# First modulation piece turned ahead of the first inverse rms, which stays in PSUM: the opening of a two-layer diffusion block

## The chip, the cores and the metric

The kernel runs on one core of one Trainium2 chip. Its engines are TensorE (PE, with PEld for its weight loads), VectorE (DVE), ScalarE (ACT), GpSimd (POOL) and SyncE (SP, which issues most transfers). The metric is the device time of one execution in microseconds; less is better.

## The reference

Two layers over 512 latent tokens and 256 context tokens of width 1024, batch 1. Only the opening of layer 0 matters here:

```
sh1, sc1, g1, sh2, sc2, g2 = split(silu(c) @ w_mod[0] + b_mod[0], 6)        # the same with c_ctx for the context
h  = rmsnorm(x,   norm_mix[0]) * (1 + sc1)  + sh1
hc = rmsnorm(ctx, norm_mix[0]) * (1 + csc1) + csh1
p  = concat(h, hc) @ w_in_ab[0]        # 1024 -> 2560, then gates and convolutions
```

All of it is float32. After the opening come the rest of the input projection, two convolutions and the output projection, the ConvFFN of layer 0, windowed attention with a sink, the ConvFFN of layer 1 and a final RMSNorm.

## The kernel before, in words

Activations lie transposed: `x` is eight tiles of 128 channels by 776 columns (512 latent, 8 empty, 256 context; `segs` are the two non-empty stretches). Every product is made three times, with each operand split into a high part (a copy in the matmul's type, by ACT) and a low part (the rest, by DVE): low weight times high activation, high times low, high times high (the three lines of `mm3`, L185 to L187 before, L188 to L190 after). `split` makes both parts, `weights` loads a 128x1024 piece of weights and splits it, `wide_gemm` multiplies a piece with the two stretches of one or more of the eight activation tiles.

PSUM is four slots of 128x1024 numbers. `start` is the opening:

- It squares and sums the eight `x` tiles (ACT and DVE). `inverse` turns the sums into means on PE (L303), reads them on ACT (`rv`) and makes the inverse root by Newton steps of small DVE instructions. DVE puts it on a diagonal (`rd`, L325) and PE spreads it over the partitions into a slot (L335).
- It makes the scale and shift of the 16 column blocks of layer 0 in four pieces. A piece (`mod_piece`) is four loads (`wmod`), 32 small matmuls into one quarter of a slot (L238), an ACT copy (`modsb`, L243), a transpose on PE (L244, here called the turn), a second ACT copy (L246), a DVE addition of the bias (`mod`, L247) and the gain (`make_gain`, L278). Piece q serves the activation tiles 2q and 2q+1.
- It normalises and modulates each tile k (`mod_in`): DVE multiplies x by the inverse rms (`xr`, L348); ACT applies gain and shift in two instructions (latent and context) and, for k of 2 and more, casts the result to the high part; DVE makes the low part. For k below 2 ACT writes the high part directly (L357) and DVE makes the full value itself (L358).
- With each tile it advances three output slots (`sl`) by three pieces of `w_in`: 18 matmuls for a tile.

The code is written in program order; a scheduling layer then lays the instructions out engine by engine, each engine executes its own list strictly in order, and semaphores carry the dependences between lists. It also orders accesses of different engines to one slot whose columns do not overlap (rows below show such waits). `issue_after` pins an instruction behind another in that layout. In the kernel before, the inverse rms goes into `sl[0]` (columns 0 to 775), is copied to SBUF (`r`, L444) by ACT, and the pieces use the fourth slot `ms` alone (`acc` at columns 0 to 127, the turn at 768 to 895).

## Time and profile before

| | |
|---|---|
| median of 3 runs | 1461.03 us (1460.87 to 1461.33) |
| the profiled execution | 1462.82 us, span of its instructions 1461.0 us |
| PE busy | 1421.9 us, 97% of the span |
| DVE, ACT, POOL busy | 74%, 44%, 12% |
| chain that ended last | PE 82%, DVE 7%, DMA 5%, ACT 3% |

The span runs from the first to the last instruction of the profiled execution. The busy share of an engine counts its instructions; the chain that ended last is followed back from the last instruction through whatever released each step. Times within the trace are counted from the start of the span.

### The profile page before, as it was taken

To read this page: it belongs to the slowest core of one execution; us is meant where nothing else is said; L and a number is where in the kernel's file an instruction comes from. 1 tells how busy PE (TensorE), PEld (TensorE's weight loads), DVE (VectorE), ACT (ScalarE), POOL (GpSimd) and SP (SyncE) were. 2 spreads that over 40 slices of the span, in tenths; PEclk is the share of its full clock that TensorE was granted. 3 is DMA by queue.
4 is the path that set the end of the run, shared out by engine and by line. 5 is a ranking of instruction groups with operands and counts; after the bars stand their busy time and mean duration, and the time that the engine had idled before them with its cause. 6 is when DMAs were issued, how large, how long until landed. Compare 5 with 4: busy or idle time off the path is not lost.

```text
span 1461.0 us, 24131 instructions
## 1 busy us (share of the span) xinstructions
PE 1421.9 (97%) x9470; PEld 1249.1 (85%) x9470; DVE 1083.3 (74%) x1750; ACT 649.8 (44%) x1105; POOL 181.3 (12%) x427
## 2 busy tenths in 40 slices
PE   5999999999999999999999999999999999999997
PEld 3888888888888888888888878867799999999897
DVE  6699998689878557565534679787767977777676
ACT  5422224473223223123213365687765745545455
POOL 0000001112222212112212110243200000000000
PEclk9999999999999999999999999999999999999999
DMA  9325433036787767847725315264532444444441
GB/s 375 113 71 174 159 116 130 30 101 204 212 223 190 218 194 197 250 156 185 162 98 100 111 59 159 67 134 110 122 116 97 157 152 158 146 156 157 148 130 68
DMA packets 80546, 215.69 MB, mean 148 GB/s; under 512 B 10032, under 2 KB 10160, under 8 KB 80304
## 3 DMA queue, kind: packets, MB, share of 16 engines
q1 hardware_dynamic: 63408, 174.29, 36.1%
q0 software_dynamic: 17024, 39.86, 13.0%
q8 instruction: 74, 1.21, 0.3%
q14 instruction: 40, 0.33, 0.1%
HBM read 209.39 MB, written 41.94 MB: 172 GB/s over the span
## 4 chain that ended last, share of the span: by engine, by line
PE 82%; DVE 7%; DMA 5%; ACT 3%; issue 2%; POOL 1%; SPq 0%; DVEq 0%; ACTq 0%
PE slot L185 20%; PE slot L186 20%; PE slot L187 19%; DMA wraw<-in_w_down 3%; PE av L1091 2%; DVE wlo L167 2%; PE pt L1081 2%; PE s L1062 2%; PE av L185 2%; PE av L186 2%; PE av L187 1%; ACT whi L166 1%; PE slot L220 1%; PE slot L224 1%; PE slot L221 1%
## 5 line engine op out<-in xcount | busy, mean ns | idle before, releaser
L185 PE MATMUL slot<-h,wlo 128*128 128x256 f32 (+1 forms) x1152 | 382.5, 334 | 2.8 <-DVE ub L582 1.2
L186 PE MATMUL slot<-h,whi 128*128 128x256 f32 (+1 forms) x1152 | 382.5, 333 | 0.2 <-DVE h L362 0.2
L187 PE MATMUL slot<-h,whi 128*128 128x256 f32 (+1 forms) x1152 | 382.7, 332 | 0.0
L166 ACT CAST whi<-wraw 128x1024 fp32r<-128x1024 f32 (+2 forms) x249 | 219.9, 892 | 240.8 <-PE slot L187 88.1
L167 DVE TENSOR_TENSOR wlo<-wraw,whi 128x1024 fp32r<-128x1024 f32 (+2 forms) x249 | 254.4, 1027 | 72.2 <-ACT whi L166 71.5
L185 PEld LDWEIGHTS slot<-h,wlo 128*128 128x128 f32 x1152 | 216.5, 188 | 29.0 <-issue 2.0
L186 PEld LDWEIGHTS slot<-h,whi 128*128 128x128 f32 x1152 | 217.0, 188 | 23.1 <-DVE h L362 0.5
L187 PEld LDWEIGHTS slot<-h,whi 128*128 128x128 f32 x1152 | 217.0, 188 | 21.8
L382 DVE SCALAR_TENSOR_TENSOR cf<-slot,par,cf 128x775 f32<-128x775 f32 (+1 forms) x92 | 92.6, 1009 | 97.8 <-ACT cf L380 97.7
L185 PE MATMUL slot<-gh,wlo 128*128 128x512 f32 (+1 forms) x435 | 148.8, 344 | 2.1 <-ACT gh L166 1.1
L186 PE MATMUL slot<-gl,whi 128*128 128x512 f32 (+1 forms) x435 | 147.9, 341 | 0.0
L187 PE MATMUL slot<-gh,whi 128*128 128x512 f32 (+1 forms) x435 | 147.6, 340 | 0.0
L380 ACT ACTIVATE cf<-slot,par 128x776 f32<-128x776 f32 (+1 forms) x46 | 41.4, 901 | 192.8 <-PE slot L187 188.7
L590 DVE SCALAR_TENSOR_TENSOR cacc<-ub,par,cacc 128x783 f32<-128x783 f32 x120 | 118.4, 1035 | 0.3
L266 DVE CUSTOM_DVE_ANT_0 junk<-wmod,cb 128x1024 bf16<-128x1024 f32 x80 | 97.5, 1218 | 22.1 <-DMA wmod<-in_wmt 20.5
L372 DVE SCALAR_TENSOR_TENSOR x<-slot,mod,x 128x256 f32<-128x256 f32 (+1 forms) x139 | 80.9, 612 | 40.9 <-PE slot L187 40.4
L185 PEld LDWEIGHTS slot<-gh,wlo 128*128 128x128 f32 x435 | 81.4, 188 | 12.7 <-ACT gh L166 1.3
L187 PEld LDWEIGHTS slot<-gh,whi 128*128 128x128 f32 x435 | 81.8, 188 | 9.8
L186 PEld LDWEIGHTS slot<-gl,whi 128*128 128x128 f32 x435 | 81.9, 188 | 9.6 <-DVE mod L247 0.2
L1069 DVE CUSTOM_DVE_ANT_0 sm<-s,mask,nsink 128x640 f32<-128x640 f32 (+1 forms) x58 | 46.6, 819 | 13.9 <-PE pt L1081 10.7
L860 ACT ACTIVATE sgf<-cf 128x776 f32<-128x776 f32 (+1 forms) x44 | 32.6, 742 | 53.6 <-DVE cf L382 53.6
L1072 ACT ACTIVATE sm<-sm,nm 128x513 f32<-128x513 f32 (+1 forms) x64 | 50.0, 785 | 10.7 <-DVE nm L1069 7.1
(333 smaller groups left out, 2873.3 us busy)
## 6 DMA issues: line engine op xcount, KB each, us to landing
s<-in_w_up POOLq DMA_DIRECT2D x114, 256.0 KB, 5.5
wmod<-in_wmt SPq DMA_DIRECT2D x56, 512.0 KB, 4.6
wraw<-in_w_up SPq DMA_DIRECT2D x50, 512.0 KB, 4.2
wmod<-in_wm SPq DMA_DIRECT2D x40, 512.0 KB, 5.1
wraw<-in_w_up SPq DMA_DIRECT2D x57, 256.0 KB, 2.9
wraw<-in_w_down SPq DMA_DIRECT2D x48, 256.0 KB, 3.1
wraw<-in_w_in SPq DMA_DIRECT2D x20, 512.0 KB, 3.9
wraw<-in_w_down SPq DMA_DIRECT2D x32, 320.0 KB, 3.0
```

Of the source, the lines that this page charges most:

```text
L166: self.act_mark = self.nc.scalar.copy(hi, src)
L167: self.mark = self.nc.vector.tensor_tensor(lo, src, hi.bitcast(F32), op=ALU.subtract)
L185: mm(out, lo, xh, start=first, stop=False)
L186: mm(out, hi, xl, start=False, stop=False)
L187: self.product = mm(out, hi, xh, start=False, stop=last)
L266: nc.vector.tensor_tensor_reduce(junk, w, self.cb[:, c, :], 1.0, 0.0, ALU.mult, ALU.add, col)
L372: self.nc.vector.scalar_tensor_tensor(self.x[k][:, lo:hi], acc, self.mod[:, l, chunk * 8 + k, c:c + 1], self.x[k][:, lo:hi], op0=ALU.mult, ...
L380: nc.scalar.activation(acc[:, :n], u[:, :n], AF.Copy, scale=w[:, 1:2])
L382: nc.vector.scalar_tensor_tensor(acc[:, o], u[:, i], w[:, j:j + 1], acc[:, o], op0=ALU.mult, op1=ALU.add)
L590: self.tapped = nc.vector.scalar_tensor_tensor(acc, ub[:, t:t + CB_N], w[:, t:t + 1], acc, op0=ALU.mult, op1=ALU.add)
L1069: scored = nc.vector.tensor_tensor_reduce(sm[:, :n], s[:, SEQ - nl:SEQ + CTX], mk, -SCALE, nsink[:, hd:hd + 1], ALU.add, ALU.min, nm)
L1072: self.scored = scored, nc.scalar.activation(sm[:, :n + 1], sm[:, :n + 1], AF.Exp, scale=-1.0, bias=nm, accum_out=z)
```

## The change

What it does, part by part:

- `mod_piece` turns into the columns that it accumulated in, 896 to 1023 of `ms`, and takes an instruction behind which its matmuls are pinned.
- The means and then the spread inverse rms lie in `ms` too, at columns 0 to 775; the copy `r` is gone, and `mod_in` reads the rms from PSUM. The spread is pinned behind the turn of piece 0.
- The first three pieces of `w_in` are no longer split in one go. ACT casts the first behind `rv` and the other two behind the second copy of piece 0. The low part of the first is made by DVE behind `rd`, that of the second by DVE between the tiles 0 and 1, that of the third by GpSimd.
- Piece 1 stands in the code behind the modulation of tile 1, piece 2 behind the products of tile 1, piece 3 behind those of tile 3. Before, piece 1 stood ahead of tile 0 and both others behind the products of tile 1.
- The products of a tile stand directly behind its modulation. Before, both tiles of a pair were modulated ahead of the products of either.

The core of the diff:

```diff
@@ -164,7 +164,10 @@
     def split(self, src, hi, lo):
 
         self.act_mark = self.nc.scalar.copy(hi, src)
-        self.mark = self.nc.vector.tensor_tensor(lo, src, hi.bitcast(F32), op=ALU.subtract)
+        self.low(src, hi, lo)
+
+    def low(self, src, hi, lo, eng=None):
+        self.mark = (eng or self.nc.vector).tensor_tensor(lo, src, hi.bitcast(F32), op=ALU.subtract)
 
     def weights(self, dram, n=1024, into=None):
...
@@ -224,7 +227,7 @@
                     self.nc.tensor.matmul(s[:, lo:hi], wh, xl, start=False, stop=k == len(rhs) - 1)
 
 
-    def mod_piece(self, l, lo, hi, at, dram, acc, tr, room):
+    def mod_piece(self, l, lo, hi, at, dram, acc, tr, room, after=None):
 
         nc = self.nc
         for quarter in range(4):
@@ -232,18 +235,19 @@
                 yield
             w = room(quarter)
             nc.sync.dma_start(w, dram[quarter])
-            for kk in range(2):
-                k = quarter * 2 + kk
-                for j in range(4):
-                    nc.tensor.matmul(
-                        acc[32 * j:32 * j + 2, :], self.csil[:, k, :], w[:, kk, j * P:(j + 1) * P],
-                        start=k == 0, stop=k == KT - 1,
-                    )
+            with self.tc.issue_after(after.ins) if after else nullcontext():
+                for kk in range(2):
+                    k = quarter * 2 + kk
+                    for j in range(4):
+                        nc.tensor.matmul(
+                            acc[32 * j:32 * j + 2, :], self.csil[:, k, :], w[:, kk, j * P:(j + 1) * P],
+                            start=k == 0, stop=k == KT - 1,
+                        )
         sb = self.tmp.tile([P, P], F32, name="modsb", tag="r", bufs=1)
         nc.scalar.copy(sb, acc)
-        nc.tensor.transpose(tr, sb, self.ident)
+        self.mod_turned = nc.tensor.transpose(tr, sb, self.ident)
         sb = self.tmp.tile([P, P], F32, name="modsb", tag="r", bufs=1)
-        nc.scalar.copy(sb, tr)
+        self.mod_copied = nc.scalar.copy(sb, tr)
         nc.vector.tensor_tensor(
...
@@ -430,31 +434,51 @@
             self.square_in(k, 0, T)
         sl = [self.slot() for _ in range(3)]
         ms = self.slot()
-        nc.vector.memset(ms[:, 0:P], 0.0)
-
-        def piece(q):
+        nc.vector.memset(ms[:, 896:1024], 0.0)
+
+        def piece(q, after=None):
             room = lambda _: ph.tile([P, 2, 512], F32, name="wmod", tag="wmod", bufs=14)
-            for _ in self.mod_piece(0, 0, 16, 2 * q, a["wm0"][q], ms[:, 0:P], ms[:, 768:768 + P], room):
+            for _ in self.mod_piece(0, 0, 16, 2 * q, a["wm0"][q], ms[:, 896:1024], ms[:, 896:1024], room, after):
                 pass
             self.make_gain(0, 0, 1, self.p("nmix")[:, 0:8], 2 * q, 2 * q + 2)
 
-        piece(0)
-        rp = self.rstd(self.ss, segs, self.ones2, sl[0], eng=nc.vector, pool=ph)
-        r = self.tmp.tile([P, T], F32, name="r", tag="ss", bufs=1)
-        nc.scalar.copy(r, rp)
-        room = [[ph.tile([P, DM], F32R, name=t) for t in ("whi0", "wlo0")], None, None]
-        first = [self.weights(a["w_in"][m], into=room[m]) for m in range(3)]
-        piece(1)
+        chunks = [c for lo, hi in segs for c in range(lo, hi, P)]
+        y = self.inverse(self.ss, chunks, self.ones2, ms[:, 0:2 * len(chunks)], nc.vector)
+        piece(0, self.stats)
+        d = ph.tile([P, len(chunks), P], F32, name="rd", tag="rd")
+        rd = nc.vector.tensor_tensor(
+            d, self.ident.unsqueeze(1).broadcast_to(d.shape), y.unsqueeze(2).broadcast_to(d.shape), op=ALU.mult)
+        with self.tc.issue_after(self.mod_turned.ins):
+            for lo, hi in segs:
+                i, j = lo // P, (hi - lo) // P
+                nc.tensor.matmul(ms[:, lo:hi], self.onesm, d[:, i:i + j, :].rearrange("p n c -> p (n c)"), start=True, stop=True)
+        r = ms[:, 0:T]
+
+        first, raws = [], []
+        for m in range(3):
+            raws.append(self.wts.tile([P, 1024], F32, name="wraw", tag="wraw", bufs=3))
+            nc.sync.dma_start(raws[m], a["w_in"][m])
+            first.append([ph.tile([P, DM], F32R, name=t) for t in ("whi0", "wlo0")] if m == 0 else
+                         [self.wts.tile([P, 1024], F32R, name=t, tag=t, bufs=3) for t in ("whi", "wlo")])
+            with self.tc.issue_after((self.mod_copied if m else self.means).ins):
+                nc.scalar.copy(first[m][0], raws[m])
+        with self.tc.issue_after(rd.ins):
+            self.low(raws[0], *first[0])
+        self.low(raws[2], *first[2], nc.gpsimd)
         h = self.new_h()
         for q in range(4):
             for k in (2 * q, 2 * q + 1):
-                self.mod_in(h, k, r, 0, 0, 0, segs)
-            for k in (2 * q, 2 * q + 1):
+                with self.tc.issue_after(self.mark.ins) if k == 1 else nullcontext():
+                    self.mod_in(h, k, r, 0, 0, 0, segs)
+                if k == 0:
+                    with self.tc.issue_after(self.mark.ins):
+                        self.low(raws[1], *first[1])
+                if k == 1:
+                    piece(1)
                 for s, w in zip(sl, first):
                     self.wide_gemm(s, w, h, segs, [k])
-            if q == 0:
-                piece(2)
-                piece(3)
+            if q < 2:
+                piece(q + 2)
         return h, sl
```

`rstd` also loses its argument `pool`, and `mod_in` calls the new `low` for k below 2.

What the layout makes of it is shown at three places. A row is an instruction of one engine in its order, with its line, result and operands, its size, and the semaphores that it waits for.

PE, from the end of piece 0 on. Before (`rd`, `onesm`: the spread; `modsb`: the turn; `wmod`: a piece's matmuls; `wlo`: a low product):

```order
L335 MATMUL slot0_102<-rd_207,onesm_86 128x512 [waits DVE_49,Activation_49]
L335 MATMUL slot0_102<-rd_207,onesm_86 128x256
L244 MATMUL slot3_105<-ident_84,modsb_177 128x128 [waits DMAHW1_49,Activation_49]
L238 MATMUL slot3_105<-wmod_231,csil_94 2x128 [waits DMAHW1_49,Activation_49]
L238 MATMUL slot3_105<-wmod_231,csil_94 2x128 x7
L238 MATMUL slot3_105<-wmod_241,csil_94 2x128 [waits DMAHW2_49]
L238 MATMUL slot3_105<-wmod_241,csil_94 2x128 x7
L238 MATMUL slot3_105<-wmod_251,csil_94 2x128 [waits DMAHW3_49]
L238 MATMUL slot3_105<-wmod_251,csil_94 2x128 x7
L185 MATMUL slot0_102<-h_278,wlo0_214 128x512 [waits Activation_49]
L185 MATMUL slot1_103<-h_278,wlo_222 128x512 [waits DVE_49]
L185 MATMUL slot2_104<-h_278,wlo_228 128x512 [waits DVE_49]
```

After:

```order
L248 MATMUL slot3_105<-ident_84,modsb_200 128x128 [waits DMAHW1_49,Activation_49]
L454 MATMUL slot3_105<-rd_207,onesm_86 128x512 [waits DVE_49,Activation_49]
L454 MATMUL slot3_105<-rd_207,onesm_86 128x256
L188 MATMUL slot0_102<-h_228,wlo0_214 128x512 [waits Activation_49]
L188 MATMUL slot2_104<-h_228,wlo_224 128x512 [waits Pool_49]
L189 MATMUL slot0_102<-h_229,whi0_213 128x512 [waits DVE_49]
L190 MATMUL slot0_102<-h_228,whi0_213 128x512
L188 MATMUL slot0_102<-h_228,wlo0_214 128x256 [waits Activation_49]
L189 MATMUL slot0_102<-h_229,whi0_213 128x256
```

The turn of piece 0 has gone ahead of the spread; the 32 matmuls of piece 1, of which 24 stood ahead of the first low product, are gone from here; the second product of tile 0 is that of the third weight piece, which waits for GpSimd.

DVE, between the low parts of the first two tiles and the later tiles (`xr_440` is tile 2, `xr_490` tile 4; after, `xr_391` and `xr_488`; `modsb_387` comes from piece 2, `modsb_484` from piece 3). Before:

```order
L362 TENSOR_TENSOR h_279<-ht_296,h_278 128x776 [waits DVE_49,Activation_49]
L348 TENSOR_TENSOR xr_440<-x2_69,r_211 128x776 [waits DMAHW2_49]
L362 TENSOR_TENSOR h_281<-ht_304,h_280 128x776 [waits DVE_49,Activation_49]
L348 TENSOR_TENSOR xr_447<-x3_70,r_211 128x776 [waits DMAHW3_49]
L247 TENSOR_TENSOR mod_92<-modsb_274,par_66 128x2x4 [waits Activation_49]
L278 SCALAR_TENSOR_TENSOR gain_93<-mod_92,par_66 128x4 [waits DVE_49]
L348 TENSOR_TENSOR xr_490<-x4_71,r_211 128x776 [waits DMAHW4_49,Activation_49]
L348 TENSOR_TENSOR xr_497<-x5_72,r_211 128x776 [waits DMAHW5_49,Activation_49]
L167 TENSOR_TENSOR h_283<-ht_442,h_282 128x776 [waits Activation_49]
L167 TENSOR_TENSOR h_285<-ht_449,h_284 128x776 [waits Activation_49]
```

After:

```order
L251 TENSOR_TENSOR mod_92<-modsb_387,par_66 128x2x4 [waits Activation_49]
L352 TENSOR_TENSOR xr_391<-x2_69,slot3_105 128x776 [waits DMAHW2_49,PE_49]
L352 TENSOR_TENSOR xr_416<-x3_70,slot3_105 128x776 [waits DMAHW3_49]
L282 SCALAR_TENSOR_TENSOR gain_93<-mod_92,par_66 128x4 [waits DVE_49]
L170 TENSOR_TENSOR wlo_605<-wraw_602,whi_604 128x1024 [waits DMAHW5_49,Activation_49]
L170 TENSOR_TENSOR h_233<-ht_393,h_232 128x776 [waits Activation_49]
L170 TENSOR_TENSOR h_235<-ht_418,h_234 128x776 [waits Activation_49]
L251 TENSOR_TENSOR mod_92<-modsb_484,par_66 128x2x4 [waits Activation_49]
L352 TENSOR_TENSOR xr_488<-x4_71,slot3_105 128x776 [waits DMAHW4_49,DVE_49,PE_49]
L352 TENSOR_TENSOR xr_513<-x5_72,slot3_105 128x776 [waits DVE_49]
```

Before, the products with the rms wait for no PE instruction and those of tiles 4 and 5 stand ahead of the `mod` of piece 2. After, those of tiles 2 and 3 stand behind the `mod` of piece 2, those of tiles 4 and 5 behind the `mod` of piece 3, and the first of each pair waits for PE.

PE, at the turn of piece 3. Before (`h_286` and `h_287` are the high and low part of tile 4) it stands among the products of tile 4:

```order
L186 MATMUL slot2_104<-h_285,whi_227 128x256
L187 MATMUL slot2_104<-h_284,whi_227 128x256
L185 MATMUL slot0_102<-h_286,wlo0_214 128x512 [waits Activation_49]
L185 MATMUL slot1_103<-h_286,wlo_222 128x512
L185 MATMUL slot2_104<-h_286,wlo_228 128x512
L244 MATMUL slot3_105<-ident_84,modsb_433 128x128 [waits Activation_49]
L186 MATMUL slot0_102<-h_287,whi0_213 128x512 [waits DVE_49]
L187 MATMUL slot0_102<-h_286,whi0_213 128x512
L185 MATMUL slot0_102<-h_286,wlo0_214 128x256
```

After (`h_235` is the low part of tile 3, `h_236` and `h_237` are tile 4):

```order
L190 MATMUL slot2_104<-h_234,whi_223 128x512
L188 MATMUL slot2_104<-h_234,wlo_224 128x256
L189 MATMUL slot2_104<-h_235,whi_223 128x256
L190 MATMUL slot2_104<-h_234,whi_223 128x256
L248 MATMUL slot3_105<-ident_84,modsb_481 128x128 [waits Activation_49]
L188 MATMUL slot0_102<-h_236,wlo0_214 128x512 [waits Activation_49]
L188 MATMUL slot1_103<-h_236,wlo_219 128x512
L188 MATMUL slot2_104<-h_236,wlo_224 128x512
L189 MATMUL slot0_102<-h_237,whi0_213 128x512 [waits DVE_49]
```

The turn now stands behind the last product of tile 3, and the first product of tile 4 is next to it.

## Rows read from the trace of the kernel before

**Rows 1.** Windows: length; busy PE, PEld, DVE, ACT, POOL (instructions); granted clock; DMA.

```profile
28.85:57.90 29.05, 29.05 (x272) 24.78 (x272) 14.04 (x21) 16.01 (x27) 0.56 (x12) 1.00 0.56 211
57.90:1461.00 1403.10, 1381.33 (x9053) 1216.73 (x9051) 1050.98 (x1688) 617.21 (x1057) 180.56 (x411) 1.00 0.48 142
```

**Rows 2.** Waits of PE from 57.9 us on: total, times, longest.

```profile
PE slot L303 <- DVE ss L296: 2.1, 2, 2.0
```

**Rows 3.** Timeline of the opening, DVE and ACT: start, length, instruction, idle before.

```profile
17.01 0.18 ACT L306 ACTIVATE rv<-slot 128x6 f32<-128x6 f32 x1 [2.54 <-PE slot L303]
...
20.72 2.17 ACT L166 CAST whi<-wraw 128x1024 fp32r<-128x1024 f32 x2
22.80 0.81 ACT L444 COPY r<-slot 128x776 f32<-128x776 f32 x1
...
20.71 3.49 DVE L167 TENSOR_TENSOR wlo<-wraw,whi 128x1024 fp32r<-128x1024 f32 x3
...
26.26 2.52 ACT L357 ACTIVATE h<-xr,mod,gain 128x512 fp32r<-128x512 f32 x4 [2.49 <-DVE gain L278]
27.84 0.96 DVE L362 TENSOR_TENSOR h<-ht,h 128x776 fp32r<-128x776 f32 x1
```

**Rows 4.** Timeline of PE in the opening.

```profile
16.90 3.59 PE L238 MATMUL slot<-wmod,csil 128*2 128x128 f32 x64
20.94 1.82 PE L335 MATMUL slot<-rd,onesm 128*128 128x512 f32 x4 [0.45 <-ACT modsb L243]
22.60 0.27 PE L244 MATMUL slot<-ident,modsb 128*128 128x128 f32 x1
...
28.85 0.50 PE L186 MATMUL slot<-h,whi 128*128 128x512 f32 x1 [0.21 <-DVE h L362]
31.41 0.85 PE L185 MATMUL slot<-h,wlo 128*128 128x512 f32 x3
34.74 1.93 PE L238 MATMUL slot<-wmod,csil 128*2 128x128 f32 x64
40.91 1.93 PE L238 MATMUL slot<-wmod,csil 128*2 128x128 f32 x64
```

**Rows 5.** Instructions of the piece matmuls and the spread: shortest, median, longest in ns.

```profile
L238 PE MATMUL slot<-wmod,csil x256: 270/273/418, 16.9 to 42.6; 128*2 128x128 f32 x128
L335 PE MATMUL slot<-rd,onesm x4: 379/486/960, 20.9 to 22.4; 128*128 128x512 f32 x2, 128*128 128x256 f32 x2
```

**Rows 6.** Timeline from the turn of piece 1 to the casts it serves, all engines.

```profile
32.10 0.27 PE L244 MATMUL slot<-ident,modsb 128*128 128x128 f32 x1
32.40 0.27 ACT L246 COPY modsb<-slot 128x128 f32<-128x128 f32 x1 [3.37 <-PE slot L244]
32.70 0.17 DVE L247 TENSOR_TENSOR mod<-modsb,par 128x8 f32<-128x8 f32 x1 [1.27 <-ACT modsb L246]
33.10 2.52 ACT L360 ACTIVATE ht<-xr,mod,gain 128x512 f32<-128x512 f32 x4 [0.43 <-DVE gain L278]
35.53 1.57 ACT L166 CAST h<-ht 128x776 fp32r<-128x776 f32 x2
```

**Rows 7.** The tile-wide instructions of that chain: shortest, median, longest in ns.

```profile
L348 DVE TENSOR_TENSOR xr<-x,r x8: 956/962/969, 24.1 to 41.2; 128x776 f32<-128x776 f32 x8
L166 ACT CAST h<-ht x6: 824/836/838, 35.5 to 50.2; 128x776 fp32r<-128x776 f32 x6
L609 DVE TENSOR_TENSOR z<-slot,gc x4: 960/965/967, 118.8 to 204.6; 128x776 f32<-128x776 f32 x4
```

**Rows 8.** The one tile-wide GpSimd instruction, and DVE's taps that started beside or behind it.

```profile
L596 POOL TENSOR_TENSOR cs<-cacc x1: 1882/1882/1882, 190.7 to 190.7; 128x783 f32<-128x783 f32 x1
L590 DVE SCALAR_TENSOR_TENSOR cacc<-ub,par,cacc x3: 1020/1021/1997, 191.5 to 194.3; 128x783 f32<-128x783 f32 x3
```

**Rows 9.** Timeline of SP's queue in the opening: the fourth and later pieces of `w_in`.

```profile
28.28 15.48 SPq L172 DMA_DIRECT2D wraw<-in_w_in  x4
```

**Rows 10.** The `wraw` tiles of the first 60 us: from issue to landing.

```profile
DMA to landing us min/median/max: 3.5/9.1/11.2
```

## What is predicted, before the run

> **What bounds the kernel now.** I read the windows first, because the change touches only the opening. From 28.85 us, the first product of a high part, to 57.90 PE is busy 29.05 us of 29.05, and after that it stands still for only 1403.10 - 1381.33 = 21.8 us in all [rows 1]; there its longest single wait is 2.0 us [rows 2], at the end of a chain that has to start later when the opening ends later. So the rest of the kernel is a line of PE work: a microsecond that PE loses or wins in the opening reaches the end, and there is hardly idle time behind it in which to lose it again. What counts is when PE can start its full run, how much of its work lies before that, and whether the run stays unbroken.
>
> The timeline of DVE and ACT shows why the run starts at 28.85. `rv` is read at 17.01; DVE then makes the inverse root, the diagonal and, from 20.71, three low parts of weights in 3.49 us, and only then, at 24.2, `xr`; ACT writes h from 26.26 and DVE its low part at 27.84 to 28.80 [rows 3]. PE meanwhile does piece 0 (16.90, 3.59 us), the spread (20.94, 1.82 us), the turn (22.60), the 32 matmuls of piece 1 in its waits, and three low products; the two later pieces, at 34.74 and 40.91, are 1.93 us of the unbroken run [rows 4].
>
> **The head of the opening.** Up to `rv`, nothing moves. The matmuls of piece 0 now wait for `rv` (17.01 + 0.18) because both lie in one slot: 17.25 instead of 16.90, and with the same 3.59 us they end at 20.85. ACT's copy (0.27, row of the turn of piece 1 [rows 6]) ends at 21.15, the turn at about 21.6 (0.27 at the pace of 22.60; I give it 0.4, since the shared pace of PE was still lower here, below), the second copy at 21.9. The spread follows at 22.0 and takes between 1.3 and the 1.82 us of [rows 4]; I take 1.5: 23.5. `xr` reads the slot; DVE products that read a slot take 965 ns against 962 without [rows 7], so reading it costs nothing and the 0.81 us copy `r` [rows 3] is saved: 24.5. ACT's two instructions for one tile are half of 2.52 us [rows 3], to 25.8; the low part takes 0.96, and with the handovers PE has its first high product at 26.9, **1.95 us earlier** than 28.85. The low part of the first weights (1.2 us of the 3.49) lies under the wait for the turn, that of the second behind the low part of tile 0, where PE has the 1.6 us of the other two slots to do.
>
> GpSimd's low part is the unknown of the head. ACT casts the second and third piece from 21.9 (2.17 us for two [rows 3]), to 24.1. The nearest row is the one tile-wide GpSimd instruction, 1882 ns for 783 columns [rows 8]: 2.46 us for 1024, so 26.6, under the 26.9. It stands second on PE, and all of PE is queued behind it. Below, the bound is DVE's own 1.2 us, which changes nothing; above, I double it, since a DVE instruction that ran beside that GpSimd row took 1997 ns instead of 1020 [rows 8] and the harm may fall on either side: 29.0, 2.1 us late. I take 2.46.
>
> The Trainium skill ("GPSIMD Engine Reference", section 8, Key points) says that GpSimd shares its SBUF interfaces with VectorE and that the two contend where VectorE reads two SBUF inputs. The 1997 ns agree; by that rule it is DVE's low part of tile 0 that stretches, by at most 1 us, and the sum would be 11.0 instead of 10.0.
>
> What PE had done by then also changes. Before, piece 1 and three low products lay ahead of the run; now it has two low products. Left over are 32 matmuls, 1.86 us (64 steps from 34.74 to 36.60 [rows 4]), and one low product, a third of 0.69 = 0.23 us (0.85 us for three with the tail [rows 4]). The head is worth -1.95 + 2.09 = **+0.15 us**: the earlier start only pays for work that used to lie in the waits.
>
> **The stalls in the run.** Before, a piece ran through behind PE's back: the turn stood among products, and `xr` of the next tiles needed nothing from PE. Now the products with the rms read `ms`, where the pieces live. The rows of the order show what follows: `xr` of tiles 2 and 3 stands on DVE behind the `mod` of piece 2, `xr` of tiles 4 and 5 behind the `mod` of piece 3, and the matmuls of pieces 1 and 3 wait for DVE.
>
> - Piece 2 waits for the second copy of piece 1, whose turn now stands directly ahead of it: turn 0.27, copy 0.27, two handovers, less the 0.13 that the turn takes of PE anyway: **0.5 us**.
> - At the end of piece 2 PE waits for its copy, turns (0.27), and waits for the second copy (0.27), `mod` (0.17) [rows 6] and two `xr` (0.96 each [rows 7]) before piece 3 may write the slot. 0.25 of tail, 0.27, 0.27, 0.27, 0.17, 1.9, with six handovers of 0.03 to 0.05 (32.37 to 32.40, 32.67 to 32.70 [rows 6]), less 0.13: **3.3 us**. Piece 3 itself (1.86) covers part of the rest of the chain: four ACT instructions 2.52, a cast 0.83 [rows 6, 7], from the end of the first `xr`, 3.3 against 0.95 + 1.86: **0.5 us**. Three low products then cover 0.69 of the 0.96 of the low part: **0.3 us**.
> - The turn of piece 3 stands behind the last product of tile 3, and the first product of tile 4 needs the whole chain from it: turn 0.27, copy 0.27, `mod` 0.17, `xr` 0.96, four ACT instructions 2.52, cast 0.83, handovers 0.15, less 0.13 = **5.0 us** in which PE has nothing, and **0.3 us** for the low part again.
>
> Tiles 5 to 7 then come in time: their ACT and DVE work per pair, 2.52 + 1.57, is less than the 6.3 us that PE needs for two tiles (29.05 us less two pieces, over eight tiles, is 3.15 for one). The sum of the stalls is 0.5 + 3.3 + 0.5 + 0.3 + 5.0 + 0.3 = 9.9 us, with the head **+10.0 us**.
>
> The Trainium skill ("PSUM — Partial Sum Buffer", section "PSUM bank collisions raise a hardware error") says that the hardware does not arbitrate between two engines in one bank and that semaphores must guard PSUM by bank rather than by address. No run here shows what the hardware does without the waits; the order shows that the waits are there although the columns are apart, which is this rule at work. If guarding went by address alone, `xr` of tiles 2 to 5 would run ahead and the sum would be about the head's 0.15.
>
> The transfers do not move: SP's list is the same, the pieces 2 and 3 are needed at about 35.5 and 41, near 34.74 and 40.91. One cast is new on the path: the fourth piece of `w_in`, ahead of ACT's work on tile 2 at 38.6. It is issued at 28.28 [rows 9] and lands at most 11.2 us later [rows 10], at 39.5; at worst it costs 0.6 us. I count nothing.
>
> Against the profiled execution the span becomes 1461.0 + 10.0; that execution took 1462.82 us, 1.8 above the median of the runs, and I make the forecast from the median: 1461.03 + 10.0 = **1471.0 us**.
>
> **Rivals.**
> - PE falls to its lower clock in the 5 us stall. The windows print a granted clock of 1.00 throughout [rows 1], but the durations show two paces: 418 ns at the start against 270 later, and 960 against 379 [rows 5]. The slower one (1.2 GHz against 2.4) is what PE had after standing still for 14.25 us, until about 21.8, the second step of the spread. No PE wait of before after that is near 5 us [rows 2], so the trace can't say whether 5 us suffice. If so, tile 4 would run at half pace, up to 3.1 us more: 1474.1. I give it 18%, since the one standstill known to have left PE slow is nearly three times as long. The Trainium skill ("TensorE: Matmul & The Clock Gate", Part 1) names the slow state the default, which follows on idleness and which activity ends.
> - GpSimd's instruction is twice as long: +2.1, 1473.1. 5%.
> - A part is given back, because ACT and DVE are ahead when PE comes late (weights of the next pieces cast in the stalls) and some of the 21.8 us of waits behind 57.90 [rows 1] shrink: half of the loss at most, 1466. 7%.
> - It is faster. The mechanism: the stalls don't reach PE, since the turn of piece 3 is done while products are still queued; then the head is all there is, with the left-over piece 1 in waits that are there anyway, 1461.0 - 1.95 = 1459.1. It decides at the turn of piece 3: it would have to run at least 5 us before the last product of tile 3 ends. The order on PE speaks against it. 4%.
> - No change, if the 9.9 us of stall are half a mis-sizing and half lie under the head's gain: within 2.9 us. 4%.
>
> **Numbers.** The forecast has 62%. A measurement of this kernel tells 0.2%, 2.9 us, from no change. Slower than 1463.95: all but the last two, 92%; same 4%, faster 4%. The range reaches from the case of a part given back to that of the clock, with a little for the cast and GpSimd, and leaves out the last two cases and the far ends: 1466.0 to 1474.8.
>
> **What would show it.** In the profile after: PE's first high product near 26.9 and tile 1 done near 34.7; a PE wait near 5 us ahead of the products of tile 4, ended by ACT's cast of h; about 3 us ahead of piece 3's matmuls, ended by DVE's `xr`; the end of the opening's products, 57.90 before, near 68; PE's busy sum unchanged but for what the clock does. Matmul durations of tile 4 near double would show the clock. Wrong would be: PE at the end of these products before 61, which means that a turn or an `xr` does not wait as the order says, or the 10 us shrinking behind it, which means that PE was not the bound there.

## The result, and the profile after

The change makes the kernel slower: 1475.89 us, median of five runs (1473.47 to 1477.37), against 1461.06 us; the ratio is 1.0096, 95% interval 1.0084 to 1.0107. The forecast was 1471.0 us with a range to 1474.8, so the direction is right and the loss too small: 14.8 us instead of 10.0. The profiled execution took 1476.52 us, its span is 1474.7 us.

The windows of the kernel after answer to those of the opening in [rows 1]: length; busy PE, PEld, DVE, ACT, POOL (instructions); granted clock; DMA share; GB/s.

```profile
27.00:31.00 4.00, 2.91 (x9) 2.53 (x10) 3.85 (x5) 0.92 (x2) 0.00 (x0) 0.54 1.02 409
31.00:35.00 4.00, 4.00 (x60) 3.11 (x61) 0.97 (x1) 0.39 (x1) 0.00 (x0) 0.61 1.03 406
...
42.00:46.00 4.00, 1.65 (x33) 1.18 (x36) 3.12 (x5) 3.74 (x7) 0.00 (x0) 0.80 0.01 2
46.00:50.00 4.00, 4.00 (x51) 2.88 (x42) 1.84 (x2) 1.73 (x3) 0.61 (x12) 0.78 0.82 295
...
58.00:62.00 4.00, 2.71 (x7) 2.19 (x8) 3.02 (x4) 3.56 (x7) 0.00 (x0) 0.50 0.00 0
62.00:66.00 4.00, 4.00 (x18) 3.44 (x17) 1.98 (x3) 3.68 (x5) 0.00 (x0) 0.64 0.00 0
```

Before, the column of the granted clock (the third from the right) read 1.00 from 28.85 us on [rows 1]. Now TensorE goes down from 2.4 to 1.2 GHz three times: near 27 us (in tile 0), near 44 (at the start of piece 3) and near 58 (ahead of tile 4); between these places and from 66 us on the column reads 1.00 again. At the very start of a run it is no guide: it reads 1.00 there in every profile, also while piece 0 takes 3.59 us [rows 4] instead of 1.93, so there the pace is taken from the durations. The PE timeline of the kernel after shows what stood ahead of each fall, as [rows 4] did before.

```profile
25.54 0.50 PE L188 MATMUL slot<-h,wlo 128*128 128x512 f32 x1 [1.90 <-ACT h L361]
26.41 0.50 PE L188 MATMUL slot<-h,wlo 128*128 128x512 f32 x1 [0.37 <-POOL wlo L170]
28.09 0.80 PE L189 MATMUL slot<-h,whi 128*128 128x512 f32 x1 [1.18 <-DVE h L170]
...
38.80 0.27 PE L248 MATMUL slot<-ident,modsb 128*128 128x128 f32 x1
39.42 1.93 PE L242 MATMUL slot<-wmod,csil 128*2 128x128 f32 x64 [0.35 <-ACT modsb L250]
...
44.41 3.54 PE L242 MATMUL slot<-wmod,csil 128*2 128x128 f32 x64 [2.35 <-issue]
...
54.28 0.27 PE L248 MATMUL slot<-ident,modsb 128*128 128x128 f32 x1
59.29 1.65 PE L188 MATMUL slot<-h,wlo 128*128 128x512 f32 x3 [4.74 <-ACT h L166]
...
75.56 0.50 PE L188 MATMUL slot<-h,wlo 128*128 128x512 f32 x1 [0.92 <-DVE ub L606]
```

The waits of the shared slot stand where they were forecast: 4.74 us between the turn of piece 3 and tile 4, 2.35 us ahead of piece 3. The trace names no releaser for the second (`issue`: the engine waited for nothing that the profile shows); DVE's two `xr`, behind which the order sets it, end at 44.31, 0.1 us before piece 3 starts:

```profile
42.48 1.83 DVE L352 TENSOR_TENSOR xr<-x,slot 128x776 f32<-128x776 f32 x2
```

Piece 3 then takes 3.54 us instead of the 1.93 of piece 2, and three low products 1.65 instead of 0.85 [rows 4]. The last row is the first product behind the gate of layer 0, which I use as the end of the opening: 75.56, against 59.32 before, so 16.24 us are lost by then. The row of before:

```profile
59.32 0.50 PE L185 MATMUL slot<-h,wlo 128*128 128x512 f32 x1 [1.15 <-DVE ub L582]
```

The timeline of DVE and POOL in the head of the kernel after:

```profile
23.67 0.96 DVE L352 TENSOR_TENSOR xr<-x,slot 128x776 f32<-128x776 f32 x1 [0.91 <-PE slot L454]
24.67 2.29 DVE L362 TENSOR_SCALAR ht<-xr,gain,mod 128x512 f32<-128x512 f32 x2
27.07 0.97 DVE L170 TENSOR_TENSOR h<-ht,h 128x776 fp32r<-128x776 f32 x1
...
30.08 0.88 DVE L362 TENSOR_SCALAR ht<-xr,gain,mod 128x512 f32<-128x512 f32 x2
...
24.00 2.36 POOL L170 TENSOR_TENSOR wlo<-wraw,whi 128x1024 fp32r<-128x1024 f32 x1 [23.54 <-ACT whi L464]
```

GpSimd's low part takes 2.36 us (forecast: 2.46). But DVE's pair of `ht` beside it takes 2.29 us, and 0.88 at 30.08 where GpSimd is idle: the pair takes 1.4 us more, and the low part of tile 0 waits for it.

**The theories.** Theory A: the loss has three parts. The waits of the shared slot; the fall of TensorE to 1.2 GHz at three places; DVE held up by GpSimd. The rivals are that one of these is not a cause (the pace, or GpSimd), or that the list of work behind the opening, which the scheduling layer lays out anew for every variant, makes the difference.

### The profile page after: what moved, and what is told of

It is laid out like the page before. It is cut to its first block, busy times and chain, and to the rows that moved or that the text cites. A ratio compares the mean times of both kernels' runs of the same rounds, so it can differ in the third digit from the quotient of the medians.

```text
span 1474.7 us, 24131 instructions
## 1 busy us (share of the span) xinstructions
PE 1426.6 (97%) x9470; PEld 1252.7 (85%) x9470; DVE 1084.4 (74%) x1749; ACT 650.5 (44%) x1104; POOL 183.8 (12%) x428
## 4 chain that ended last, share of the span: by engine, by line
PE 84%; DVE 7%; DMA 3%; ACT 3%; issue 2%; POOL 1%; SPq 0%; DVEq 0%; ACTq 0%
PE slot L188 20%; PE slot L189 20%; PE slot L190 20%; PE av L1115 2%; PE pt L1105 2%; DMA wraw<-in_w_down 2%; PE s L1086 2%; PE av L189 2%; PE av L188 2%; PE av L190 2%; DVE wlo L170 2%; PE slot L242 1%; PE pt L188 1%; PE pt L190 1%; PE pt L189 1%
## 5 line engine op out<-in xcount | busy, mean ns | idle before, releaser
L166 ACT CAST whi<-wraw 128x1024 fp32r<-128x1024 f32 (+2 forms) x246 | 216.8, 890 | 236.5 <-PE slot L190 92.0
L725 POOL COPY tk<-cf 128x1 f32<-128x1 f32 x41 | 19.4, 473 | 285.7 <-DVE cf L386 252.7
```

The costliest lines, as they stand in the source:

```text
L166: self.act_mark = self.nc.scalar.copy(hi, src)
```

## The experiments

**1. The shared slot taken back.** One thing is undone: `r` lies in SBUF again.

```diff
-        r = ms[:, 0:T]
+        r = self.tmp.tile([P, T], F32, name="r", tag="ss", bufs=1)
+        nc.scalar.copy(r, ms[:, 0:T])
```

> The changed kernel with one thing taken back: ACT copies the inverse rms out of PSUM again, so no xr reads the slot of the pieces. Theory A (pieces and inverse rms in one slot make PE stand still about 10 us, and TensorE falls to 1.2 GHz in these stalls, about 6 more): the waits of 4.74 us ahead of tile 4 and 2.35 us ahead of piece 3 are gone, tiles 2 to 4 and the pieces 2 and 3 run at 0.39 us for 512 columns and 1.93 us for a piece, and the time is 1462 to 1467 us; what is left over 1461 is GpSimd's low part and the copy of 0.8 us. Rival B (the loss lies in the head and in work that moved, not in the slot): still 1471 us or more.

Measured: 1465.14 us, ratio to before 1.0025 (1.0015 to 1.0035). The PE timeline of this kernel has no wait ahead of the later pieces, and its longest ones are these:

```profile
28.01 0.73 PE L188 MATMUL slot<-h,wlo 128*128 128x512 f32 x2 [1.42 <-ACT h L361]
...
55.84 0.96 PE L188 MATMUL slot<-h,wlo 128*128 128x512 f32 x3 [1.35 <-ACT h L166]
63.85 0.50 PE L188 MATMUL slot<-h,wlo 128*128 128x512 f32 x1 [1.15 <-DVE ub L607]
```

The opening ends 4.5 us late instead of 16.2; from 27 us on the granted clock is 1.00 in all its windows, and three low products take 0.96 us. That is theory A: 11 of the 15 us hang on the slot, the falls of the clock included. DVE met GpSimd here too, now with an `xr` that reads two operands from SBUF (timeline of DVE, the same kernel): 2.52 us instead of 0.96.

```profile
24.59 2.52 DVE L352 TENSOR_TENSOR xr<-x,r 128x776 f32<-128x776 f32 x1 [2.10 <-ACT r L456]
```

**2. GpSimd's low part given to DVE,** all else as in the changed kernel.

```diff
-        self.low(raws[2], *first[2], nc.gpsimd)
...
                         self.low(raws[1], *first[1])
+                        self.low(raws[2], *first[2])
```

> The changed kernel, with the low part of the third weights made by DVE behind that of the second, not by GpSimd. Theory A (DVE's pair of ht was stretched by the GpSimd instruction beside it, 2.29 us instead of 0.88, which costs 1.4 us in the head): the pair takes 0.88 us, the low part of tile 0 starts about 1.4 us earlier than 27.07; but DVE has 1.2 us more to do ahead of tile 1, so the time changes by -1.4 to +1 us from 1475.9. Rival B (the 2.29 us come from something else, as the PSUM read or the state of tile 0): the pair stays near 2.3 us. Rival C (GpSimd's part is what costs the extra 5 us over the forecast): 1471 us.

Measured: 1477.51 us (1475.71 to 1478.36), ratio 1.011 (1.0096 to 1.0124). In DVE's timeline the pair is short again:

```profile
24.70 0.87 DVE L362 TENSOR_SCALAR ht<-xr,gain,mod 128x512 f32<-128x512 f32 x2
```

The low part of tile 0 starts at 26.04, one microsecond earlier, so GpSimd is what stretched the pair; rivals B and C fall. TensorE falls in tile 0 all the same, and the total doesn't gain: the wait ahead of piece 3 grows from 2.35 to 3.74 us, because the new layout puts the cast of the next weights (ACT, 39.69, 1.05 us) ahead of piece 2's second copy and their low part (DVE, 40.77, 1.23 us) ahead of `mod`.

**3. The stall ahead of tile 4 filled.** TensorE gets work that nobody waits for, pinned behind the turn of piece 3; the matmuls add into unused columns.

```diff
+        nc.vector.memset(sl[0][:, T:T + 240], 0.0)
...
                 piece(q + 2)
+                if q == 1:
+                    with self.tc.issue_after(self.mod_turned.ins):
+                        for _ in range(10):
+                            nc.tensor.matmul(
+                                sl[0][:, T:T + 240], self.onesm, self.x[0][:, 0:240], start=False, stop=False,
+                                skip_group_check=True)
```

> The changed kernel with ten fp32 products of 240 columns into unused columns of a slot (about 4 us of TensorE work at 2.4 GHz), ready from the turn of piece 3 on, in the stall ahead of tile 4; nothing waits for them. Theory A (TensorE falls to 1.2 GHz because it stands still there for 4.74 us): tile 4 starts at the same time, 59.3, and runs at 0.39 us for 512 columns instead of 0.63, the granted clock is 1.00 at 58 to 66 us, and the time is about 2.6 us lower: 1473.3 us. Rival B (tile 4 is slow for another reason, as its operands or the DMA): no change, 1475.9 us. Rival C (the difference of the opening does not reach the end): tile 4 fast, time unchanged.

Measured: 1476.36 us (1475.73 to 1477.83), ratio 1.0105 (1.0089 to 1.012). Its PE timeline has the fill, tile 4 and the end of the opening:

```profile
52.47 4.21 PE L486 MATMUL slot<-x,onesm 128*128 128x240 f32 x20
57.37 0.96 PE L188 MATMUL slot<-h,wlo 128*128 128x512 f32 x3 [0.69 <-ACT h L166]
...
71.57 0.50 PE L188 MATMUL slot<-h,wlo 128*128 128x512 f32 x1 [0.92 <-DVE ub L613]
```

Three low products take 0.96 us, not 1.65, and from the turn of piece 3 to the end of the opening it is 19.2 us instead of 21.3: the standstill is what makes tile 4 slow, and against the first profile of the changed kernel that costs 2.1 us. The opening as a whole ended 4.0 us earlier, since one of the other falls was missing and one shorter in this execution. The total did not follow, which looks like rival C; but the rest behind the opening took 1403.3 us, against 1399.1 in the changed kernel. In ACT's timeline a cast near the end waits 3.15 us for a weight:

```profile
1439.95 0.73 ACT L166 CAST th<-wraw 128x640 fp32r<-128x640 f32 x1 [3.15 <-DMA wraw<-in_w_down]
```

In the changed kernel the same cast waited 1.23 us. That is 1.9 of the 4.2 us that the rest grew by; where the others arose is not shown. Experiment 9 tries whether this is bound to the list.

**4. The shared slot alone,** put into the kernel before.

```diff
-        nc.vector.memset(ms[:, 0:P], 0.0)
+        nc.vector.memset(ms[:, 896:1024], 0.0)
...
-            for _ in self.mod_piece(0, 0, 16, 2 * q, a["wm0"][q], ms[:, 0:P], ms[:, 768:768 + P], room):
+            for _ in self.mod_piece(0, 0, 16, 2 * q, a["wm0"][q], ms[:, 896:1024], ms[:, 896:1024], room):
...
-        rp = self.rstd(self.ss, segs, self.ones2, sl[0], eng=nc.vector, pool=ph)
-        r = self.tmp.tile([P, T], F32, name="r", tag="ss", bufs=1)
-        nc.scalar.copy(r, rp)
+        r = self.rstd(self.ss, segs, self.ones2, ms, eng=nc.vector, pool=ph)
```

> The kernel before, in which alone the products of the inverse rms go to the slot of the pieces and stay there (no copy, pieces in the last 128 columns); all low parts on DVE in the old code order. The layout then also sets the matmuls of piece 0 and the means apart. Theory A (sharing the slot is the whole loss): 1472 to 1478 us, with waits of 2 to 3 us ahead of piece 3 and near 5 us ahead of tile 4, and slow TensorE behind the latter. Rival B (the new order in the head or GpSimd is the loss): 1461 to 1465 us.

Measured: 1479.7 us (1475.24 to 1480.41; the profile is of the shortest), ratio 1.012 (1.0106 to 1.0134). GpSimd has no part in it. In its PE timeline the slot makes the means wait for piece 0 (they start at 20.29 instead of 14.25), so that the root comes late to the spread, and tile 2 waits for piece 3:

```profile
20.29 2.72 PE L303 MATMUL slot<-ones,ss 128*128 128x2 f32 x12 [0.64 <-ACT modsb L246]
27.53 2.90 PE L335 MATMUL slot<-rd,onesm 128*128 128x512 f32 x4 [4.52 <-DVE rd L325]
...
51.97 1.65 PE L185 MATMUL slot<-h,wlo 128*128 128x512 f32 x3 [4.71 <-ACT h L166]
```

The slot alone costs as much as the whole change or more, and a little more than expected. It does so in part by another way: the pieces still follow each other here, so of the two long waits one stands ahead of the spread and one ahead of tile 2, and the 6.6 us by which the spread is late are a loss that the changed kernel, with piece 0 behind the means, does not have.

**5 and 6. Both kernels once more,** unaltered.

> The changed kernel unaltered, a second profile of it beside the same of the kernel before. In the first profile 16.24 us were lost up to the first product behind the gate of layer 0 (75.56 against 59.32), but only 13.7 at the end. Theory A (the 2.5 us that come back lie in events that differ from one execution to the next, as where TensorE falls to 1.2 GHz): the same list gives a rest, from that product to the end, that differs from 1399.1 us by 1 us or more, and the falls of the clock in the opening need not be the same three. Rival B (the list of the changed kernel is shorter to run behind the opening): 1399.1 us again, within 0.3.

> The kernel before unaltered, a second profile. In the first the rest from the first product behind the gate of layer 0 to the end took 1401.7 us. Theory A (chance of the execution): a rest that differs from this by 1 us or more, near 1399 to 1400. Rival B (a property of its list): 1401.7 again, within 0.3.

Measured: 1475.89 us (ratio 1.0102, 1.0086 to 1.0117) and, for the kernel before, 1462.90 us in a single run. The windows of the second profile of the changed kernel show two falls, not three:

```profile
27.00:31.00 4.00, 3.30 (x12) 2.87 (x13) 3.52 (x5) 1.31 (x2) 0.00 (x0) 0.57 1.03 410
...
42.00:46.00 4.00, 2.92 (x68) 2.14 (x68) 2.76 (x5) 3.82 (x7) 0.61 (x12) 1.00 0.29 79
...
54.00:58.00 4.00, 1.32 (x3) 1.01 (x4) 3.33 (x6) 3.56 (x7) 0.00 (x0) 0.56 0.00 0
```

In its PE timeline piece 3 keeps the full pace behind the same wait; the second row is the end of the opening:

```profile
42.61 1.93 PE L243 MATMUL slot<-wmod,csil 128*2 128x128 f32 x64 [2.35 <-issue]
...
72.52 0.50 PE L189 MATMUL slot<-h,wlo 128*128 128x512 f32 x1 [0.92 <-DVE ub L607]
```

The opening ended at 72.52 instead of 75.56 with the same list and the same waits (2.35 and 4.74 us). So the wait ahead of piece 3 makes TensorE fall in one execution and not in another. The rest behind the opening took 1399.9 us (1399.1 in the first profile), and 1401.6 in the kernel before (1401.7): in two profiles of each, the rest repeats within 0.8 and 0.1 us. For the kernel before rival B holds. For the changed kernel neither theory has the rest quite (0.7 us lies between 0.3 and 1), but the falls differ, as theory A said they might.

**7. GpSimd's low part alone,** put into the kernel before.

The part of the edit that gives `split` its separate `low`, as in the changed kernel, is left out here.

```diff
-        first = [self.weights(a["w_in"][m], into=room[m]) for m in range(3)]
+        first = [self.weights(a["w_in"][m], into=room[m]) for m in range(2)]
+        raw = self.wts.tile([P, 1024], F32, name="wraw", tag="wraw", bufs=3)
+        nc.sync.dma_start(raw, a["w_in"][2])
+        first.append([self.wts.tile([P, 1024], F32R, name=t, tag=t, bufs=3) for t in ("whi", "wlo")])
+        nc.scalar.copy(first[2][0], raw)
+        self.low(raw, *first[2], nc.gpsimd)
```

> The kernel before, in which alone the low part of the third weights is made by GpSimd; the lists of TensorE, ACT and SP stay word for word the same, DVE's has one instruction less. Theory A (while GpSimd runs its 2.36 us, DVE's instructions on SBUF alone don't get on): GpSimd starts near 24, and DVE's xr of tile 0, or the ht behind it, takes about 2.3 us instead of 0.96, so the 1.2 us that DVE saves are lost again and the first high product stays within 0.5 us of 28.85. Rival B (no contention): xr 0.96, ht 0.88 for a pair, first high product near 27.7. In both the time is 1460 to 1462 us, since TensorE has its list to get through anyway.

Measured: 1463.94 us (1462.12 to 1465.02), ratio 1.0016 (1.0008 to 1.0025): 2.5 us slower, where both theories had no change. The timeline of DVE, POOL and PE in the head:

```profile
23.63 3.39 DVE L351 TENSOR_TENSOR xr<-x,r 128x776 f32<-128x776 f32 x2 [0.56 <-ACT r L447]
...
22.97 2.35 POOL L170 TENSOR_TENSOR wlo<-wraw,whi 128x1024 fp32r<-128x1024 f32 x1 [22.52 <-ACT whi L453]
...
28.20 1.65 PE L188 MATMUL slot<-h,wlo 128*128 128x512 f32 x3 [1.88 <-ACT h L360]
```

The same in the kernel before (DVE, PE):

```profile
24.12 1.83 DVE L348 TENSOR_TENSOR xr<-x,r 128x776 f32<-128x776 f32 x2
...
27.13 0.97 PE L185 MATMUL slot<-h,wlo 128*128 128x512 f32 x3 [0.81 <-ACT h L357]
```

Two `xr` take 3.39 us instead of 1.83: theory A on DVE. What it left out is PE: the wait ahead of the low products grows from 0.81 to 1.88 us, and they run at the slow pace. The windows of this kernel show the granted clock go with it:

```profile
24.00:27.00 3.00, 1.66 (x48) 0.76 (x40) 3.00 (x3) 0.00 (x0) 1.32 (x1) 1.00 1.02 407
27.00:31.00 4.00, 2.80 (x20) 1.50 (x21) 3.93 (x10) 2.59 (x5) 0.00 (x0) 0.57 1.02 405
31.00:35.00 4.00, 4.00 (x16) 3.47 (x17) 1.49 (x2) 0.20 (x1) 0.00 (x0) 0.58 1.03 410
```

One microsecond of delay (ACT's first h at 27.33, not 26.26) becomes 3.5 us at the end of the opening (62.83), through the clock: PE has no further wait from 28.20 to 35 us, where the column reads 1.00 again. PE's list is that of the kernel before, word for word, so nothing else is left to explain it.

**8. Piece 3 back behind piece 2,** the slot still shared.

```diff
-            if q < 2:
-                piece(q + 2)
+            if q == 0:
+                piece(2)
+                piece(3)
```

> The changed kernel with piece 3 behind piece 2 again, both behind the products of tile 1, the shared slot kept. Theory A (each pass of a piece through the slot of the inverse rms makes the tiles behind it wait for the turn, two copies, xr and the modulation): the stalls of 2.35 us ahead of piece 3 and 4.74 us ahead of tile 4 are replaced by one of about 5 us ahead of tile 2 and three of 0.6, TensorE falls to 1.2 GHz once less, and the time is 2 to 4 us lower, 1472 to 1474 us. Rival B (the place of the pieces in the list is the loss, not the slot): 1461 to 1465 us.

Measured: 1473.27 us (1472.47 to 1474.29), ratio 1.0081 (1.0068 to 1.0095). PE's timeline shows the stalls merge as theory A had it:

```profile
41.86 1.93 PE L242 MATMUL slot<-wmod,csil 128*2 128x128 f32 x64 [0.36 <-ACT modsb L250]
...
49.22 1.65 PE L188 MATMUL slot<-h,wlo 128*128 128x512 f32 x3 [4.71 <-ACT h L166]
```

TensorE falls twice, as expected. The place of the pieces decides how many long waits there are, and is worth 2.6 us at the medians (its opening ended at 71.48; the intervals of the two ratios still overlap); the slot decides that there are any.

**9. The fill of experiment 3 with another list behind it:** `range(12)` and 200 columns.

```diff
+        nc.vector.memset(sl[0][:, T:T + 200], 0.0)
...
+                        for _ in range(12):
+                            nc.tensor.matmul(
+                                sl[0][:, T:T + 200], self.onesm, self.x[0][:, 0:200], start=False, stop=False,
+                                skip_group_check=True)
```

> The fill of the stall ahead of tile 4 once more, with 12 products of 200 columns in place of ten of 240: as much TensorE work, but behind the opening the layout gives another list. With ten of 240 the opening ended 4.0 us earlier than in the changed kernel's first profile, yet the rest took 1403.3 us instead of 1399.1, with one weight landing 2.2 us late near the end. Theory A (the fill saves the clock's share, and that late weight belongs to that list): tile 4 at full pace, rest 1399 to 1400 us, time 1472 to 1474 us. Rival B (what the fill saves is lost again behind the opening whatever the list): 1475 to 1477 us.

Measured: 1475.02 us (1472.97 to 1475.52), ratio 1.009 (1.0077 to 1.0104). Tile 4 again runs at the full pace (three low products 0.96 us), the late weight is gone (that cast waits 1.43 us), but the rest is 1401.2 us, still 2.1 more than in the changed kernel. The total lies at the lower end of rival B, and its interval holds the changed kernel's ratio: that the fill helps the total is not shown. In this execution TensorE also rose later at the start (the spread took 2.93 us, 1.56 in the changed kernel), so its first tile was slow without a fall.

One more thing can be seen in its timelines of DVE and GpSimd: `xr`, with one operand in PSUM, starts while GpSimd's low part is under way and takes its usual time.

```profile
25.19 0.96 DVE L352 TENSOR_TENSOR xr<-x,slot 128x776 f32<-128x776 f32 x1 [2.62 <-PE slot L455]
...
24.14 2.35 POOL L170 TENSOR_TENSOR wlo<-wraw,whi 128x1024 fp32r<-128x1024 f32 x1 [23.69 <-ACT whi L465]
```

**10. All three costs taken back:** the copy of experiment 1, the low part of 2, the pieces of 8; what stays of the change is the early turn of piece 0 and the later low parts.

> The changed kernel with its three costs taken back and the rest kept: ACT copies the inverse rms to SBUF, DVE makes the third low part (behind the second), and piece 3 follows piece 2 behind the products of tile 1; the early turn of piece 0 and the later low parts stay. Theory A (slot, GpSimd and the place of piece 3 are all of the loss): 1460 to 1462.5 us, TensorE at 2.4 GHz through the opening, no wait over 1.5 us from 22 us to the gate. Rival B (the early turn or the later low parts cost something of their own): 1464 us or more.

Measured: 1465.51 us (1463.03 to 1466.37), ratio 1.0027 (1.0017 to 1.0038). Rival B by the number. PE's timeline suggests why:

```profile
22.13 2.93 PE L454 MATMUL slot<-rd,onesm 128*128 128x512 f32 x4 [0.35 <-ACT modsb L250]
25.95 2.74 PE L242 MATMUL slot<-wmod,csil 128*2 128x128 f32 x48 [0.90 <-ACT r L456]
...
62.10 0.50 PE L188 MATMUL slot<-h,wlo 128*128 128x512 f32 x1 [1.15 <-DVE ub L608]
```

There are no stalls, but the spread takes 2.93 us, where it took 1.82 before [rows 4], and the piece matmuls of piece 1 run at the slow pace: by these durations TensorE had not yet risen to 2.4 GHz. The opening ends 2.8 us late. The next two runs test the late rise.

**11 and 12. TensorE kept busy during the loads of x,** in the kernel before and in that of experiment 10; the products go to columns that nobody reads.

```diff
         ms = self.slot()
+        for k in range(KT):
+            for _ in range(2 if k < 7 else 7):
+                nc.tensor.matmul(sl[0][:, 784:1024], self.onesm, self.x[k][:, 0:240], start=True, stop=True)
```

> The kernel before, with 21 fp32 products of 240 columns on TensorE while it waits for the loads of x (two for each of the first seven tiles, seven for the last), into unused columns of a slot. Theory A (TensorE is at 1.2 GHz for the means and piece 0 because it has stood still for 14.25 us): the 12 matmuls of the means take about 1.4 us instead of 2.72 and piece 0 about 1.9 instead of 3.59, the root starts 1.3 us earlier, and the opening ends up to 1.3 us earlier; the three low parts and the loads still bind behind it, so the time is 1459.5 to 1461.5 us. Rival B (the pace of these small matmuls is not the clock's): 2.72 and 3.59 as before, time unchanged or later if the fill outlasts the wait.

> The changed kernel with its three costs taken back (inverse rms copied to SBUF, third low part by DVE, piece 3 behind piece 2) and the same fill during the loads of x. Without the fill it took 1465.5 us against 1461.35, with TensorE at its slow pace until 29.7 us in the profile where the kernel before rises at 21.5. Theory A (what is left of the loss is the late rise of TensorE's clock, since the early turn leaves it less to do in the head): the spread takes about 1.5 us instead of 2.93, piece 1 its 1.9, and the time falls by 2 to 5 us, to 1460.5 to 1463 us. Rival B (the early turn or the later low parts cost it): 1465 us as before.

Measured: 1460.96 us (ratio 0.9997, 0.9988 to 1.0006) and 1462.44 us (ratio 1.0007, 0.9998 to 1.0016). PE's timeline of the former:

```profile
4.29 11.47 PE L435 MATMUL slot<-x,onesm 128*128 128x240 f32 x42 [4.29 <-DMA x<-in_x]
15.60 1.40 PE L303 MATMUL slot<-ones,ss 128*128 128x2 f32 x12
16.93 1.93 PE L238 MATMUL slot<-wmod,csil 128*2 128x128 f32 x64
```

Means 1.40 us instead of 2.72 and piece 0 1.93 instead of 3.59 [rows 4]: the pace is the clock's. The fill held the means up: they start at 15.60, where they started at 14.25 before, which ate the gain, so the time stays.

In the kernel of experiment 10 the fill brings the spread to 1.53 us, and of the 4.2 us that it took longer than the kernel before 0.7 are left, or 1.5 when both have the fill. By the total that is theory A. But its profile does not bear out the way: the opening ended at 61.38, only 0.7 us earlier than in experiment 10 (62.10), since TensorE now fell in tile 0,

```profile
27.00:31.00 4.00, 4.00 (x31) 2.71 (x34) 4.00 (x5) 1.20 (x2) 0.00 (x0) 0.60 1.03 410
```

and the rest behind the opening took 1399.3 us instead of 1402.4. So it is shown that the late rise slows the head of experiment 10, and not that it is what its time had left of the loss. None of these beats the kernel before by more than can be measured.

## Why the prediction fell short

The sum can be checked in four terms, in the two profiles of the changed kernel. Times are those of the first high product, the turn of piece 1, the turn of piece 3 and the end of the opening; the last two columns are kernels with the stall ahead of tile 4 filled.

| | after | after, again | exp. 3 | exp. 9 |
|---|---|---|---|---|
| first high product | 28.09 | 27.70 | 28.09 | 28.55 |
| to the turn of piece 1 | 10.71 | 9.29 | 9.55 | 9.91 |
| to the turn of piece 3 | 15.48 | 14.68 | 14.72 | 14.67 |
| to the end of the opening | 21.28 | 20.85 | 19.21 | 19.20 |

- **The stalls and the left-over work were right.** At full pace the three stretches take 7.7 (an estimate: two tiles of 3.15, less two low products of 0.23, with piece 1 of 1.86), 14.7 and 19.2 us, 41.6 in all; before, it was 30.47 from 28.85 to 59.32. The difference is 11.1, and the steps had 9.9 + 2.09 = 12.0. No profile shows the first stretch at full pace from end to end, so the 7.7, and with it the border between this term and the clock's share of tile 0, remains an estimate.
- **The start of the run was wrong by about 1 us.** Forecast -1.95, found -0.76 and -1.15 (in the first profile 0.55 us of what is missing is that the means themselves start at 14.80 instead of 14.25). The step that failed is GpSimd's: its duration was right, but the sum let it lie "under the 26.9" and kept DVE's stretching out, which the text named as possible (11.0 instead of 10.0), and for another instruction: the low part of tile 0, not the pair of `ht` ahead of it. GpSimd held that pair up by 1.4 us; the other steps of the head came 0.5 to 0.8 us earlier than summed.
- **The clock is the term that was mis-sized.** The rival that "PE falls to its lower clock in the 5 us stall" was given 18% and at most 3.1 us, because the one standstill known to leave PE slow was 14.25 us. It happened in both profiles, and in experiments 2, 4 and 8 too: in all five profiles with a wait of 4.7 us in the run, three low products behind it took 1.65 us. The upper end of the range allowed for this one fall. And it was not confined to that stall: the waits of the head (1.90, 0.37 and 1.18 us, with 0.5 us of products between) bring a fall in both, the 2.35 us ahead of piece 3 in one. Against the full pace that is 3.0 + 0.8 + 2.1 = 5.9 us in the first profile and 1.6 + 0 + 1.6 = 3.2 in the second.
- **The sums:** -0.76 + 11.1 + 5.9 = 16.2, where 16.24 was read, and -1.15 + 11.1 + 3.2 = 13.15, where it was 13.20. They must close, since they are made of the same stretches; what they show is the size of each term. That the miss stayed at 4.8 us is in part luck: the stalls came out 0.9 us smaller than forecast, and the rest behind the opening some 2 us shorter.
- **"Given back" did not decide it.** Between the profiled executions 2.5 us of the 16.24 were missing at the end: the rest took 1399.1 and 1399.9 us in the changed kernel, 1401.6 and 1401.7 in that of before. But over the fourteen profiles the rest, 1399.1 to 1403.3 us, does not follow how late the opening ended: it was 1399.5 in experiment 11 (59.59) and 1403.3 in experiment 3 (71.57). What makes one rest shorter than another stays open; it was not tried, and a difference of two or three us between the totals of kernels with different lists says little about their openings. Both profiled executions of the kernel before (1462.82 and 1462.90) lie some 1.5 us above the median of its runs. Against that median those of the changed kernel lost 15.5 and 13.1 us, and the median loss, 14.8, lies between them.
- **The rule on slots held.** `xr` waited for pieces in other columns of the slot, as the order shows, and experiment 1 takes these waits away with the slot.

The Trainium skill ("TensorE: Matmul & The Clock Gate", Part 1) calls the slow state the default, to which idleness leads. The trace agrees, with 0.50 granted at 58 us after 4.74 us of standing still; experiment 7 shows that several waits below 2 us can do it as well. The Trainium skill ("SBUF — State Buffer", section "Who interferes with whom") says that of a GpSimd and a DVE instruction that need the shared pair of ports, the first has it for its whole length and the other blocks. The trace agrees: GpSimd, which had started first, ended at 26.36 and the pair of `ht` 0.60 us later; in experiment 1 GpSimd ended at 26.29 and `xr` at 27.11. By that rule, and with the 0.60, the sum would have had the low part of tile 0 at 26.6 + 0.6 = 27.2 instead of 25.8, and so 1.4 us where it took "at most 1"; it was found at 27.07.

## What to carry to other kernels

Saving a copy by leaving a value in PSUM can be dear when other engines' traffic shares its slot: each later pass through the slot joins three engines into one chain in which TensorE has nothing. Price a TensorE wait with the work that may run at half pace behind it, short waits too, and give it a range, since one list falls in one execution and not in the next. And before GpSimd takes work from DVE, look at what DVE does in those microseconds.

## What the runs showed of the hardware that was not expected

- A fall of TensorE's clock needs no long standstill. In experiment 7 waits of 1.24, 0.66 and 1.88 us, with short products between them, were enough, and a delay of 1 us became 3.5 us. In the kernel before, 0.95, 0.66, 0.81 and 0.21 us at the same place were not, nor 1.25, 0.66, 0.79 and 0.21 us in its second profile. With the fill at the start 1.31, 1.89, 0.23 and 0.63 us were not enough in experiment 11, and 1.06, 1.49, 0.63 and 0.45 us were in experiment 12. So the lengths alone don't tell, and the same list fell three times in one execution and twice in another.
- The rise can be late too: with waits ahead of it the spread took 2.93 us in experiment 10, and 1.53 with TensorE busy from 4.2 us on.
- GpSimd's 2.36 us stopped DVE's fp32 `tensor_scalar` with a single SBUF tensor (2.29 us for 0.88) just as it stopped a product of two SBUF tensors (2.52 for 0.96), but not the same product with one operand in PSUM (in experiment 9 0.96 us from 25.19 on, with GpSimd at work from 24.14 to 26.49). GpSimd's own time was the same in all four: 2.36, 2.36, 2.35 and 2.35 us.
